# A two-layer conformer and attention trunk with grouped experts: the order of routing picks, of large experts' up splits, and GpSimd's share beside the routing

## The chip, the cores and the metric

The kernel runs on 1 core of a Trainium2 chip, as one program. Its time is the device time in microseconds, taken as the median of several runs. Five engines work side by side, each in the order of its own queue: TensorE (PE, with its weight loads as PEld), VectorE (DVE), ScalarE (ACT), GpSimd (POOL) and SyncE (SP), which only issues transfers and reads registers here. An instruction waits at the head of its engine's queue until its inputs are there, and everything queued behind it on that engine waits too.

## The reference, cut to what matters

512 tokens of width 1024 go through two layers. Each layer has a token mixer (layer 0: a conformer convolution; layer 1: differential attention over keys and values that are projected once) and then a mixture of 16 experts, of which each token uses two. Every part ends with a residual sum and a layer norm.

```
for l in range(2):
    mix = conformer_conv(x, ...) if l == 0 else diff_attention(x, k1, k2, v, ...)
    x = layer_norm(ALPHA * x + mix, ln_mix_g[l], ln_mix_b[l])
    # grouped_moe
    aff = sigmoid(x @ router_w); sel = aff + router_bias      # 4 groups of 4 experts
    group = argmax(sum of the two best sel of each group)
    e_idx = the two best experts of that group
    gates = one_hot(e_idx) * aff / (sum of the two aff)
    for e in range(16):
        h = silu(x @ w_gate[e]) * (x @ w_up[e])
        out += (h @ w_down[e]) * gates[:, e]
    x = layer_norm(ALPHA * x + out, ln_ffn_g[l], ln_ffn_b[l])
```

All inputs and the output are float32. Each expert's three weight matrices are 2 MB each.

## The kernel before, in words

**Precision.** Products that need it are made from two parts: a weight or an activation in float32 is split into a high part `hi` (a copy on ScalarE, L280) and a low part `lo` (the difference, on VectorE, L281), and a product is three matmuls (`mm3`, L283 to L286): hi by hi, hi by lo, lo by hi.

**Tiling.** Tokens are handled in four rows of 128 (`NT`). Layer 0's mixer ends in the product pw2, layer 1's in `project_out`; both accumulate a row of 128 x 1024 in two PSUM banks. `rows_out` (L1035 on) then adds the residual (L1040), transposes for the router (L1047), takes the logits (L1055), the statistics (L1062 to L1068), normalizes the row (L1084) and writes it out. For the last row, its first half is normalized by ScalarE and GpSimd instead (L1072 to L1081).

**Routing.** `route_tasks` (L352 on) computes for each row, in some 15 short VectorE instructions, which experts a token takes (`msk`), and with small matmuls (L395, L396) the place of each token in its expert's list (`pos`). Then `select_tasks` (L425 on) makes a one-hot matrix (L429) and TensorE picks expert 0's tokens out of the normalized rows: per row and half four matmuls (L439), accumulated over the four rows in banks 0 and 1; in total eight picks. The result is split to `xT0` (L1028, L1032), the input of expert 0. After the last row, `order_tasks` (L459 on) ranks the experts by their counts (`cnt`, L406; L467 to L477), and two small products (L481, L482) spread the order over all partitions, where VectorE copies it to `pii`, `pi` and `over` (L484 to L488). SP reads `pii` to find the weights of experts from the fourth on. `gates` (L411 to L415) are five VectorE steps that turn affinities into gate values; `arrange` (L492 on) uses them inside the expert stage.

**Who orders the mixers and the routing.** They are written as tasks of a planner (`Plan`, L109 on). A task has an engine, an estimated cost, what it reads and writes, and a priority. The planner takes the task that can begin first by its own estimates and, of those that can begin at once, the one with the lowest priority number; the engines' queues then hold that order. A pick is planned at 0.86 us (1.76 us with the zeroing of its bank), with priority 0; a mixer product at 0.645 to 1.29 us with priority 2. `first_parts` (L1099 on) splits the first two pieces of expert 0's gate weight within the plan, high parts on ScalarE (L1111) and low parts on GpSimd (L1112).

**Experts.** `moe` (L606 on) handles the experts in order of their counts. Experts 3, 5, 7, 9, 11 and 13 are small (64 places, unsplit float32 products); the others are large. A large expert: its gate product (`first_part`, with the transposes of the expert before it between its two halves), Silu, its up product (`product`, 24 matmuls), the multiplication, the transposes, the down product, a scaled copy to `y`, and a scatter from GpSimd that adds `y` to memory. There is one `y` buffer (`Y_BUFS = 1`). Weight splits use four `hi` and four `lo` buffers, just those of one weight. For a small expert e and the large one behind it, the order in the text is: gate product of e + 1, then small expert's down product with its copy to `y` and its scatter (`small_out`, L874 on: L879, L881, L882), then, in the next turn of the loop, the up weight of e + 1 is split and multiplied. Weights come as pieces of 1 MB through SP's queue (L251), at most three under way, up to 15 buffers ahead.

Of the kernel before, what the change touches and what calls it, by code (L numbers as in the profile page):

```python
# [11 lines left out]
F32 = mybir.dt.float32  # L12
# [4 lines left out]
ALU = mybir.AluOpType  # L17
# [178 lines left out]
def trunk(ctx: ExitStack, tc, x, a_w_pw1, a_b_pw1, a_w_dw, a_b_dw, a_ln_g, a_ln_b, a_w_pw2, a_b_pw2,  # L196
# [155 lines left out]
    def route_tasks(plan, b, R, room):  # L352
# [48 lines left out]
        if last:  # L401
            def total():
                for c in range(NT):
                    PE.matmul(pc[:, NT], ones16, msk[:, c], start=(c == 0), stop=(c == NT - 1))
            plan.add("PE", .2, total, [("route", c) for c in done], [("pc", NT)], 1)
            plan.add("DVE", .07, lambda: V.tensor_copy(R["cnt"], pc[:, NT, None, :].to_broadcast([P, 2, E])), [("pc", NT)], ["cnt"], 2)  # L406
            order_tasks(plan, R)
            g, m1 = o1, t4("gm1", [P, NT, 1])

            def gates():  # L410
                V.tensor_tensor(g, aff, msk, op=ALU.mult)  # L411
                V.tensor_reduce(m1, g, axis=AX.X, op=ALU.add)
                V.reciprocal(m1, m1)
                V.tensor_scalar(m1, m1, 1.0 / ALPHA, None, op0=ALU.mult)
                V.tensor_tensor(R["pg"][:, :, 1], g, m1.to_broadcast([P, NT, E]), op=ALU.mult)  # L415
            plan.add("DVE", 1.0, gates, [("route", c) for c in done], ["gates"], 9)
            plan.add("ACT", 1.3, lambda: A.activation(cp.tile([P, 1], F32, tag="sgl", name=nm("sgl")), aff[:, b, 0:1],
                                                      AF.Silu), [rk], ["table"], 3)
# [6 lines left out]
    def select_tasks(plan, b, R, z, zk, banks, late):  # L425
# [6 lines left out]
        for h in range(2):  # L432
            def pick(h=h):
# [4 lines left out]
                for j in range(4):  # L438
                    PE.matmul(banks[h][0][:, j], v[:, j], late["oh0"][:, b], start=False,  # L439
                              stop=(k == NT - 1 and j == 3))  # L440
            plan.add("PE", .86 + .9 * (k == 0), pick, [("oh", b), (zk, 0), (zk, 1)], [banks[h][1]], 0)
        plan.add("DVE", .2, lambda: V.tensor_tensor(
            late["oh1"][:, b], iota1, R["pos"][:, b, 1:2].to_broadcast([P, P]), op=ALU.is_equal),
            [("route", b), "late"], [("oh1", b), ("aT", 1), "rel"])
        if k == NT - 1:
# [8 lines left out]
            for h in range(2):  # L454
                ks = slice(4 * h, 4 * h + 4)
                split_tasks(plan, *(Later(lambda i=i, ks=ks: R["xT0"][:, i, ks]) for i in range(2)), banks[h][0], 512,
                            ("xT0", 0, h), ("xT0", 1, h), [banks[h][1], "xT0"])

    def order_tasks(plan, R):  # L459
# [20 lines left out]
        def arranged():  # L480
            PE.matmul(place_, ecol[0:E].to_broadcast([E, P]), hot[0:E, 0:E], start=True, stop=True)  # L481
            PE.matmul(of, kc[0:E, 1:2].to_broadcast([E, P]), hot[0:E, 0:E], start=True, stop=True)  # L482
        plan.add("PE", .4, arranged, ["hot"], [("pc", "pi")], 0)
        plan.add("DVE", .15, lambda: V.tensor_copy(pii, place_), [("pc", "pi")], ["pii"], 1)  # L484

        def rest():
            V.tensor_copy(pi, place_)
            V.tensor_tensor(over, of, caps, op=ALU.subtract)  # L488
        plan.add("DVE", .3, rest, [("pc", "pi")], ["pi"], 8)
        R.update(hot=hot, pi=pi, pii=pii, over=over)  # L490

# [114 lines left out]
    def moe(l, R, xsrc, ydst, more, order, first):  # L606

        with ExitStack() as st:
# [264 lines left out]

            def small_out(w, hs, yo, ixcol, gcol):  # L874
                acc = bank([P, 512])
                wd = [r.rearrange("p a b -> p (a b)").rearrange("p (j d) -> p j d", j=2) for r in w]
                for k in range(4):
                    for n in range(2):
                        PE.matmul(acc[64 * n:64 * (n + 1)], hs[:, k], wd[k // 2][:, k % 2, 512 * n:512 * (n + 1)],  # L879
                                  start=(k == 0), stop=(k == 3))  # L880
                A.activation(yo, acc, AF.Copy, scale=gcol)  # L881
                G.indirect_dma_start(out=half_view(ydst), out_offset=bass.IndirectOffsetOnAxis(ap=ixcol, axis=0),  # L882
# [82 lines left out]

            first_part(0)
            find_rows([0, 2], ohs)
            for e in range(E):
# [36 lines left out]
                if e in SMALL:  # L1005
                    small_out(weight(2, e), hT[e], new_y()[:, 512:1024], rows[e], gate[e])
                elif e < E - 1:
# [27 lines left out]
    def rows_out(plan, l, b, z, zk, acc, turned, logit, rx, norm, last=False):  # L1035
# [34 lines left out]
        for n in range(2):  # L1070
            zv = lambda n=n: z[:, zs[n]]
            if last and n == 0:  # L1072
                add("DVE", .07, lambda: V.scalar_tensor_tensor(
                    norm["nr"], norm["mv", b][:, 0:1], -1.0, norm["rs", b], op0=ALU.mult, op1=ALU.mult), [nk], ["nr"])
                add("ACT", .6, lambda zv=zv: A.activation(zv(), zv(), AF.Identity, scale=norm["rs", b][:, 0:1],
                                                          bias=norm["nr"][:, 0:1]), ["nr"], [(zk, n)], 1)

                def rest(zv=zv, n=n):
                    G.tensor_tensor(zv(), zv(), norm["g"][:, zs[n]], op=ALU.mult)
                    G.tensor_tensor(zv(), zv(), norm["b"][:, zs[n]], op=ALU.add)  # L1080
                add("POOL", 2.6, rest, ["ln_g", "ln_b"], [(zk, n)], 1)  # L1081
                continue
            for k, at, op in (("g", lambda: norm["mv", b], ALU.subtract), ("b", lambda: norm["rs", b], ALU.mult)):
# [15 lines left out]
    def first_parts(plan, pieces):  # L1099

        for i in range(2):
            for u in range(4):
                def part(k, u=u, i=i):
# [6 lines left out]
                    if not k:  # L1110
                        return A.activation(hi, src, AF.Copy)  # L1111
                    return G.tensor_tensor(lo, src, hi.bitcast(F32), op=ALU.subtract)  # L1112
                keys = [("hi", i, u // 2), ("lo", i, u // 2)]
                plan.add("ACT", .5, lambda part=part: part(0), [], [("raw", i), *keys], 3)
                plan.add("POOL", 1.25, lambda part=part: part(1), [], [("raw", i), keys[1]], 3)

# [884 lines left out]
```

## Time and profile before

| | |
|---|---|
| median of 3 runs | 1209.08 us (1207.22 to 1209.73) |
| profiled execution | 1207.24 us, span from first to last instruction 1205.5 us |
| PE busy | 1085.8 us (90%) |
| DVE busy | 786.0 us (65%) |
| ACT busy | 585.7 us (49%) |
| POOL busy | 323.6 us (27%) |
| mean granted TensorE clock | 0.954 |

A busy TensorE is not TensorE at its peak: matmuls are pipelined and their ends are modelled. The granted clock is the share of the full 2.4 GHz that TensorE was given; 0.5 is its lower level. In a timeline row stand the start and the duration in us, the engine, the line of the kernel, the operation, what it writes and reads, how many instructions were merged, and in brackets the idle time of the engine just before, with what ended it. By stages: layer 0's convolution runs to about 200 us, its routing to 264, its experts to about 560; the attention runs from there to about 847, its routing to 866, and layer 1's experts to about 1180.

### The profile page before, as it was taken

What the parts mean: (1) busy time and instruction counts of PE and PEld (TensorE: products, weight loads), DVE (VectorE), ACT (ScalarE), POOL (GpSimd) and SP (SyncE); (2) the same over time, 40 slices, a digit from 0 to 9 for tenths busy, and PEclk for the clock granted to TensorE, in tenths of its full rate; (3) what the DMA queues carried; (4) which work ended last, traced back from release to release, by engine and by line L of the source; (5) the groups of instructions that cost most, each with busy time, mean ns of one, the idle gap of its engine ahead of it and who ended that gap; (6) DMA issues with size and microseconds to landing.
All of it is one profiled execution on the core that took longest, in us unless ns stands there. A gap on an engine that the chain in (4) does not pass through costs nothing. (4 is left out here: it accounts for less than half of the span.)

```text
span 1205.5 us, 14628 instructions
## 1 busy us (share of the span) xinstructions
PE 1085.8 (90%) x5053; PEld 786.4 (65%) x5053; DVE 786.0 (65%) x1396; ACT 585.7 (49%) x932; POOL 323.6 (27%) x261
## 2 busy tenths in 40 slices
PE   6999769979999999967899999999699999898965
PEld 5888658867656665555677787688576556545632
DVE  4899974568866655467647738665598665544637
ACT  4556433137655545464346636542276555444631
POOL 2999941231112222012401101012311122110113
PEclk9999969979999999978999999999799999998998
DMA  8620335768999999958451131444589999999223
GB/s 249 208 71 1 138 108 87 276 225 286 360 361 366 372 372 385 389 186 262 151 146 36 36 105 71 175 140 164 193 314 356 393 386 375 381 395 383 81 71 125
DMA packets 80818, 276.58 MB, mean 229 GB/s; under 512 B 9691, under 2 KB 38725, under 8 KB 56150
## 3 DMA queue, kind: packets, MB, share of 16 engines
q1 hardware_dynamic: 72326, 259.44, 58.7%
q0 software_dynamic: 8256, 15.95, 5.6%
q8 instruction: 45, 0.74, 0.2%
q14 instruction: 47, 0.39, 0.1%
q10 hardware_dynamic: 144, 0.07, 0.0%
HBM read 258.62 MB, written 27.00 MB: 237 GB/s over the span
## 5 line engine op out<-in xcount | busy, mean ns | idle before, releaser
L281 DVE TENSOR_TENSOR lo<-raw,hi 128x1024 fp32r<-128x1024 f32 x232 | 280.3, 1230 | 121.5 <-ACT hi L280 118.8
L280 ACT ACTIVATE hi<-raw 128x1024 fp32r<-128x1024 f32 x236 | 244.7, 1058 | 86.6 <-PE mm L286 85.9
L284 PE MATMUL mm<-hi,xgh 128*128 128x512 f32 x288 | 122.0, 424 | 29.1 <-ACT hi L280 13.4
L285 PE MATMUL mm<-lo,xgh 128*128 128x512 f32 x288 | 119.3, 414 | 4.6 <-DVE lo L281 4.5
L286 PE MATMUL mm<-hi,xgl 128*128 128x512 f32 x288 | 118.0, 410 | 0.0
L1032 DVE TENSOR_TENSOR lo<-raw,hi 128x1024 fp32r<-128x1024 f32 x45 | 66.4, 1479 | 62.9 <-ACT hi L1028 62.3
L284 PE MATMUL all<-xh,hi 128*128 128x512 f32 x256 | 102.2, 399 | 0.2 <-ACT xh L1028 0.2
L285 PE MATMUL all<-xl,hi 128*128 128x512 f32 x256 | 99.9, 390 | 1.1 <-DVE xl L1032 1.1
L286 PE MATMUL all<-xh,lo 128*128 128x512 f32 x256 | 99.9, 390 | 0.0
L733 POOL DMA_INDIRECT ys<-y,ix x18 | 30.0, 1668 | 242.8 <-ACT y L732 189.3
L848 PE MATMUL mm<-raw,xgl 128*64 128x512 f32 x384 | 90.9, 599 | 0.0
L284 PEld LDWEIGHTS mm<-hi,xgh 128*128 128x128 f32 x288 | 56.7, 197 | 48.4 <-ACT hi L280 18.6
L1424 POOL TENSOR_TENSOR yconv<-yconv,prod 128x512 f32<-128x512 f32 x60 | 86.5, 1443 | 5.1 <-ACT yconv L1414 2.2
L1407 DVE SCALAR_TENSOR_TENSOR all<-hglu,wT,all 128x512 f32<-128x512 f32 x122 | 84.5, 752 | 2.6 <-ACT all L1393 1.8
L1421 ACT ACTIVATE prod<-hglu,wT 128x512 f32<-128x512 f32 x60 | 42.9, 721 | 60.0 <-POOL yconv L1424 54.7
L1810 POOL TENSOR_TENSOR fs<-fs,mhalf 128x1 f32<-128x1 f32 x32 | 19.4, 607 | 187.3 <-DVE fs L1808 187.1
L285 PEld LDWEIGHTS mm<-lo,xgh 128*128 128x128 f32 x288 | 56.6, 196 | 18.7 <-DVE lo L281 7.3
L286 PEld LDWEIGHTS mm<-hi,xgl 128*128 128x128 f32 x288 | 56.5, 196 | 16.1 <-DVE xgl L281 3.7
L286 PE MATMUL mm<-hi,hTl 128*128 128x512 f32 x160 | 63.9, 402 | 0.8 <-DVE hTl L281 0.8
L284 PE MATMUL mm<-hi,hTh 128*128 128x512 f32 x160 | 62.7, 411 | 1.5 <-ACT hTh L280 1.4
L285 PE MATMUL mm<-lo,hTh 128*128 128x512 f32 x160 | 64.0, 400 | 0.0
L1028 ACT ACTIVATE hi<-raw 128x1024 fp32r<-128x1024 f32 x52 | 54.3, 1054 | 12.9 <-DMA raw<-in_a_w_pw 10.0
(359 smaller groups left out, 2179.7 us busy)
## 6 DMA issues: line engine op xcount, KB each, us to landing
raw<-in_moe_w_gate SPq DMA_DIRECT2D x64, 1024.0 KB
raw<-in_moe_w_up SPq DMA_DIRECT2D x64, 1024.0 KB
raw<-in_moe_w_down SPq DMA_DIRECT2D x64, 1024.0 KB
raw<-in_a_w_pw SPq DMA_DIRECT2D x10, 1024.0 KB
raw<-in_w_kv SPq DMA_DIRECT2D x4, 1024.0 KB
raw<-in_w_kv SPq DMA_DIRECT2D x8, 512.0 KB
raw<-in_b_w_q SPq DMA_DIRECT2D x8, 512.0 KB
raw<-in_b_w_o SPq DMA_DIRECT2D x4, 1024.0 KB
```

The costliest lines, as they stand in the source:

```text
L280: nxt["high"] = A.activation(hi, src, AF.Copy).ins
L281: nxt["low"] = low.tensor_tensor(lo, src, hi.bitcast(F32), op=ALU.subtract).ins
L284: PE.matmul(acc, sh, mh, start=first, stop=False)
L285: PE.matmul(acc, sh, ml, start=False, stop=False)
L286: return PE.matmul(acc, sl, mh, start=False, stop=last).ins
L733: G.indirect_dma_start(out=ydst[:, :], out_offset=bass.IndirectOffsetOnAxis(ap=ixcol, axis=0), in_=y, in_offset=None, bounds_check=T - 1, ...
L848: PE.matmul(acc[at_:at_ + 64], xs[:, j, 64 * h:64 * (h + 1)], wm[h][:, j], start=(k == 0), stop=(k == KC - 1))
L1028: A.activation(now(hi), src, AF.Copy)
L1032: lambda: eng.tensor_tensor(now(lo), src, now(hi).bitcast(F32), op=ALU.subtract), sk + [hk], [lk],
L1407: add("DVE", .663, lambda v=v, dst=dst, src=src: V.scalar_tensor_tensor(dst, h[:, c, v:v + T], wT[:, c, v:v + 1], src, op0=ALU.mult, op1=A ...
L1421: add("ACT", .61, lambda v=v, p=p: A.activation(prod[p], h[:, c, v:v + T], AF.Copy, scale=wT[:, c, v:v + 1]), hk + wk, [("prod", p)], PRI[ ...
L1424: add("POOL", 1.3, lambda p=p: G.tensor_tensor(y[c], y[c], prod[p], op=ALU.add), [("prod", p)], [("y", c)], PRI["add"])
```

## The change

- `small_out` gets an instruction behind which its copy to `y` is issued. Where a small expert is followed by a large one, the large one's up weight is loaded and split (`halves_in`) just before `small_out`, and the copy is issued behind the last high part. The loop's later `product(weight(1, e), ...)` finds the split parts in `ahead`.
- The picks' priority goes from 0 to 3, below the mixer products' 2.
- The copy of the counts has priority 0 instead of 2.
- The gates' task is added behind the last split of `xT0` and waits for it.
- The two small products of `order_tasks` and the three copies behind them leave the plan; they are issued between the two halves of expert 0's gate product.
- The last row's first half is normalized by VectorE like every other half, and the low parts in `first_parts` are made by VectorE (priority 7) instead of GpSimd.

```diff
--- before.py
+++ after.py
@@ -403,7 +403,7 @@
                 for c in range(NT):
                     PE.matmul(pc[:, NT], ones16, msk[:, c], start=(c == 0), stop=(c == NT - 1))
             plan.add("PE", .2, total, [("route", c) for c in done], [("pc", NT)], 1)
-            plan.add("DVE", .07, lambda: V.tensor_copy(R["cnt"], pc[:, NT, None, :].to_broadcast([P, 2, E])), [("pc", NT)], ["cnt"], 2)
+            plan.add("DVE", .07, lambda: V.tensor_copy(R["cnt"], pc[:, NT, None, :].to_broadcast([P, 2, E])), [("pc", NT)], ["cnt"], 0)
             order_tasks(plan, R)
             g, m1 = o1, t4("gm1", [P, NT, 1])
 
@@ -413,7 +413,7 @@
                 V.reciprocal(m1, m1)
                 V.tensor_scalar(m1, m1, 1.0 / ALPHA, None, op0=ALU.mult)
                 V.tensor_tensor(R["pg"][:, :, 1], g, m1.to_broadcast([P, NT, E]), op=ALU.mult)
-            plan.add("DVE", 1.0, gates, [("route", c) for c in done], ["gates"], 9)
+            R["gating"] = lambda: plan.add("DVE", 1.0, gates, [("route", c) for c in done] + [("xT0", 1, 1)], ["gates"], 9)
             plan.add("ACT", 1.3, lambda: A.activation(cp.tile([P, 1], F32, tag="sgl", name=nm("sgl")), aff[:, b, 0:1],
                                                       AF.Silu), [rk], ["table"], 3)
 
@@ -438,7 +438,7 @@
                 for j in range(4):
                     PE.matmul(banks[h][0][:, j], v[:, j], late["oh0"][:, b], start=False,
                               stop=(k == NT - 1 and j == 3))
-            plan.add("PE", .86 + .9 * (k == 0), pick, [("oh", b), (zk, 0), (zk, 1)], [banks[h][1]], 0)
+            plan.add("PE", .86 + .9 * (k == 0), pick, [("oh", b), (zk, 0), (zk, 1)], [banks[h][1]], 3)
         plan.add("DVE", .2, lambda: V.tensor_tensor(
             late["oh1"][:, b], iota1, R["pos"][:, b, 1:2].to_broadcast([P, P]), op=ALU.is_equal),
             [("route", b), "late"], [("oh1", b), ("aT", 1), "rel"])
@@ -455,6 +455,7 @@
                 ks = slice(4 * h, 4 * h + 4)
                 split_tasks(plan, *(Later(lambda i=i, ks=ks: R["xT0"][:, i, ks]) for i in range(2)), banks[h][0], 512,
                             ("xT0", 0, h), ("xT0", 1, h), [banks[h][1], "xT0"])
+            R["gating"]()
 
     def order_tasks(plan, R):
 
@@ -480,13 +481,12 @@
         def arranged():
             PE.matmul(place_, ecol[0:E].to_broadcast([E, P]), hot[0:E, 0:E], start=True, stop=True)
             PE.matmul(of, kc[0:E, 1:2].to_broadcast([E, P]), hot[0:E, 0:E], start=True, stop=True)
-        plan.add("PE", .4, arranged, ["hot"], [("pc", "pi")], 0)
-        plan.add("DVE", .15, lambda: V.tensor_copy(pii, place_), [("pc", "pi")], ["pii"], 1)
-
-        def rest():
+        def places():
+            arranged()
+            V.tensor_copy(pii, place_)
             V.tensor_copy(pi, place_)
             V.tensor_tensor(over, of, caps, op=ALU.subtract)
-        plan.add("DVE", .3, rest, [("pc", "pi")], ["pi"], 8)
+        R["places"] = places
         R.update(hot=hot, pi=pi, pii=pii, over=over)
 
     def arrange(R, bank, room):
@@ -871,14 +871,15 @@
                 A.activation(hs, pt, AF.Copy)
                 return hs
 
-            def small_out(w, hs, yo, ixcol, gcol):
+            def small_out(w, hs, yo, ixcol, gcol, after=None):
                 acc = bank([P, 512])
                 wd = [r.rearrange("p a b -> p (a b)").rearrange("p (j d) -> p j d", j=2) for r in w]
                 for k in range(4):
                     for n in range(2):
                         PE.matmul(acc[64 * n:64 * (n + 1)], hs[:, k], wd[k // 2][:, k % 2, 512 * n:512 * (n + 1)],
                                   start=(k == 0), stop=(k == 3))
-                A.activation(yo, acc, AF.Copy, scale=gcol)
+                with tc.issue_after(after) if after else ExitStack():
+                    A.activation(yo, acc, AF.Copy, scale=gcol)
                 G.indirect_dma_start(out=half_view(ydst), out_offset=bass.IndirectOffsetOnAxis(ap=ixcol, axis=0),
                                      in_=yo, in_offset=None, bounds_check=2 * T - 1, oob_is_err=False,
                                      compute_op=ALU.add)
@@ -963,7 +964,7 @@
                 else:
                     sg[e] = gated(weight(0, e), xT[e], between)
 
-            first_part(0)
+            first_part(0, R["places"])
             find_rows([0, 2], ohs)
             for e in range(E):
                 if e + 1 < E:
@@ -1003,7 +1004,11 @@
                     with tc.issue_after(turned_x):
                         beyond_first(R, mp)
                 if e in SMALL:
-                    small_out(weight(2, e), hT[e], new_y()[:, 512:1024], rows[e], gate[e])
+                    wd, after = weight(2, e), None
+                    if e + 1 not in SMALL:
+                        ahead[1, e + 1] = halves_in(weight(1, e + 1))
+                        after = nxt["high"]
+                    small_out(wd, hT[e], new_y()[:, 512:1024], rows[e], gate[e], after)
                 elif e < E - 1:
                     expert_out(weight(2, e), *hT[e], rows[e], gate[e])
                 else:
@@ -1069,17 +1074,6 @@
         add("DVE", .3, lambda: negated_logits(l, lg[:, b], pl, norm["mv", b], norm["rs", b]), [nk, lk], [("lg", b)])
         for n in range(2):
             zv = lambda n=n: z[:, zs[n]]
-            if last and n == 0:
-                add("DVE", .07, lambda: V.scalar_tensor_tensor(
-                    norm["nr"], norm["mv", b][:, 0:1], -1.0, norm["rs", b], op0=ALU.mult, op1=ALU.mult), [nk], ["nr"])
-                add("ACT", .6, lambda zv=zv: A.activation(zv(), zv(), AF.Identity, scale=norm["rs", b][:, 0:1],
-                                                          bias=norm["nr"][:, 0:1]), ["nr"], [(zk, n)], 1)
-
-                def rest(zv=zv, n=n):
-                    G.tensor_tensor(zv(), zv(), norm["g"][:, zs[n]], op=ALU.mult)
-                    G.tensor_tensor(zv(), zv(), norm["b"][:, zs[n]], op=ALU.add)
-                add("POOL", 2.6, rest, ["ln_g", "ln_b"], [(zk, n)], 1)
-                continue
             for k, at, op in (("g", lambda: norm["mv", b], ALU.subtract), ("b", lambda: norm["rs", b], ALU.mult)):
                 add("DVE", .66, lambda zv=zv, n=n, k=k, at=at, op=op: V.scalar_tensor_tensor(
                     zv(), zv(), at()[:, 0:1], norm[k][:, zs[n]], op0=op, op1=ALU.mult if k == "g" else ALU.add),
@@ -1109,10 +1103,10 @@
                     src = raw_of[i][:, u]
                     if not k:
                         return A.activation(hi, src, AF.Copy)
-                    return G.tensor_tensor(lo, src, hi.bitcast(F32), op=ALU.subtract)
+                    return V.tensor_tensor(lo, src, hi.bitcast(F32), op=ALU.subtract)
                 keys = [("hi", i, u // 2), ("lo", i, u // 2)]
                 plan.add("ACT", .5, lambda part=part: part(0), [], [("raw", i), *keys], 3)
-                plan.add("POOL", 1.25, lambda part=part: part(1), [], [("raw", i), keys[1]], 3)
+                plan.add("DVE", .66, lambda part=part: part(1), [], [("raw", i), keys[1]], 7)
 
     raw_of = {}
```

## Rows read from the trace of the kernel before

**Rows 1.** Page, busy time by engine, and transfer engines' busy tenths in 40 slices.

```profile
PE 1085.8 (90%) x5053; PEld 786.4 (65%) x5053; DVE 786.0 (65%) x1396; ACT 585.7 (49%) x932; POOL 323.6 (27%) x261
...
DMA  8620335768999999958451131444589999999223
```

**Rows 2.** Stretches: length, busy us (instructions) by engine, granted clock, DMA share, GB/s.

```profile
222.46:241.60 19.14, 19.14 (x95) 16.72 (x93) 9.31 (x19) 4.83 (x9) 6.62 (x6) 1.00 0.58 218
241.60:263.61 22.01, 13.78 (x73) 13.06 (x73) 17.65 (x48) 5.87 (x10) 11.39 (x10) 0.69 0.79 287
846.65:865.96 19.31, 8.39 (x55) 7.80 (x55) 14.62 (x42) 5.25 (x9) 8.78 (x8) 0.71 0.67 228
```

**Rows 3.** Timeline of TensorE, two up products behind a small expert.

```profile
514.38 0.79 PE L284 MATMUL mm<-hi,xgh 128*128 128x512 f32 x1 [3.11 <-ACT hi L280]
...
1126.94 0.50 PE L284 MATMUL mm<-hi,xgh 128*128 128x512 f32 x1 [1.78 <-ACT hi L280]
```

**Rows 4.** Timeline of ScalarE, small experts' copies to y, and one run of splits.

```profile
346.78 0.69 ACT L881 ACTIVATE y<-mm,sgate 128x512 f32<-128x512 f32 x1 [2.25 <-PE mm L879]
...
512.70 0.69 ACT L881 ACTIVATE y<-mm,sgate 128x512 f32<-128x512 f32 x1 [4.38 <-DMA ys<-y,ix]
513.28 3.89 ACT L280 ACTIVATE hi<-raw 128x1024 fp32r<-128x1024 f32 x4
...
1046.05 0.69 ACT L881 ACTIVATE y<-mm,sgate 128x512 f32<-128x512 f32 x1 [4.99 <-DMA ys<-y,ix]
...
1086.98 0.69 ACT L881 ACTIVATE y<-mm,sgate 128x512 f32<-128x512 f32 x1 [6.81 <-DMA ys<-y,ix]
...
1125.26 0.69 ACT L881 ACTIVATE y<-mm,sgate 128x512 f32<-128x512 f32 x1 [3.05 <-PE mm L879]
```

**Rows 5.** Stretches of five up products of large experts, columns as in rows 2.

```profile
511.27:523.36 12.09, 8.51 (x25) 6.49 (x26) 5.86 (x5) 7.65 (x9) 1.56 (x1) 0.72 0.81 291
1043.80:1055.08 11.28, 7.75 (x26) 5.41 (x25) 3.50 (x3) 4.01 (x5) 2.64 (x2) 0.85 1.00 368
1083.11:1097.14 14.03, 8.02 (x26) 5.78 (x24) 4.63 (x4) 4.47 (x5) 1.59 (x1) 0.76 1.01 380
1125.16:1135.20 10.04, 7.50 (x26) 5.85 (x26) 5.86 (x5) 7.65 (x8) 1.55 (x1) 0.83 0.09 11
947.34:953.12 5.78, 5.78 (x27) 4.39 (x26) 2.65 (x3) 4.06 (x5) 2.62 (x2) 1.00 1.01 375
```

**Rows 6.** Timeline of TensorE in the two routing stages.

```profile
231.01 3.77 PE L439 MATMUL all<-oh,xt 128*128 128x128 f32 x16
...
263.07 0.39 PE L481 MATMUL all<-rank,cs 16*128 16x16 f32 x2 [1.99 <-DVE rank L477]
...
263.61 0.50 PE L284 MATMUL mm<-hi,xT 128*128 128x512 f32 x1
...
857.39 0.17 PE L396 MATMUL all<-msk,tri 128*128 128x16 f16 x1 [6.96 <-DVE msk L387]
```

**Rows 7.** Timeline of VectorE in the two routing stages.

```profile
241.59 1.20 DVE L371 TENSOR_TENSOR before<-gs 128x16 f32<-128x16 f32 x1
...
246.89 0.74 DVE L1084 SCALAR_TENSOR_TENSOR xt<-xt,ln_mv,g 128x512 f32<-128x512 f32 x1
...
252.27 1.23 DVE L381 TENSOR_TENSOR sel<-aff,rb 128x16 f32<-128x16 f32 x1
...
254.73 0.17 DVE L371 TENSOR_TENSOR before<-gs 128x16 f32<-128x16 f32 x1
...
853.63 1.30 DVE L374 TENSOR_TENSOR before<-before,cs 128x64 f32<-128x64 f32 x1
```

**Rows 8.** ScalarE's waits from 890 to 1130 us, grouped: total, times, longest.

```profile
ACT hi L280 <- PE mm L286: 18.9, 40, 1.2
```

**Rows 9.** Timeline of SP's queue, loads of two up weights.

```profile
489.26 2.83 SPq L251 DMA_DIRECT2D raw<-in_moe_w_up  x2
...
1054.44 3.46 SPq L251 DMA_DIRECT2D raw<-in_moe_w_up  x2
```

## The prediction

> **What bounds the kernel now.** I read the page first. TensorE is busy for 90% of the span, and the transfer engines show nines in both expert stages [rows 1]. So two resources could set the pace there, and gaps on TensorE are worth something only where no load sets it. Next I cut the span into stretches: in the two stages where a layer is routed, TensorE is busy 13.78 of 22.01 us and 8.39 of 19.31 us, at a granted clock of 0.69 and 0.71; just ahead of the first it is busy 19.14 of 19.14 us at 1.00 [rows 2]. The reader is to see three different limits in a row: TensorE full, then a chain of short VectorE steps, then experts. Inside the experts I listed what TensorE waits for. Four waits stand out, all at the first up product of a large expert behind a small one, all for ScalarE's high part of the up weight (the first and the last of them: [rows 3]). ScalarE's own row just ahead names the cause [rows 4]: it stood at the small expert's copy (L881), in three cases for the scatter of the previous `y` (one buffer), in the fourth for TensorE's own small product. The first row of that group is one of the eight other places of this kind: there the copy waits 2.25 us for the small product, and TensorE lost nothing.
>
> **The up splits ahead of the copy.** Removed: the four waits. The price of each is read over a whole up product of 24 matmuls, because the clock also falls afterwards: 12.09, 11.28, 14.03 and 10.04 us, at granted clocks of 0.72 to 0.85, against 5.78 us at 1.00 for the undisturbed one [rows 5]. The excesses are 6.31, 5.50, 8.25 and 4.26, together 24.3 us. Behind the change ScalarE goes from the gate's Silu straight to four splits (3.89 us for the four [rows 4]), and only then to the copy. The gate product has by then read all four hi and lo buffers, so the splits wait for nothing. In the first case they would begin at about 508.3 and the first low part would be done near 510.6, before TensorE ends the small product at 511.27. What is late next: the copy itself still waits for its scatter until 512.70, 1046.05 and 1086.98 [rows 4], and behind it on ScalarE stand the splits of the next weight. Those need buffers that the up product begins to give back a quarter of 5.78 us after its start, so they lose up to 2 to 3 us, but they are wanted only when the up product and, twice, two small products are through. I take 2 us off for this: 22 us. Bounds: 0 (the wait moves with the copy) to 24.3. In the eight other places the copy comes about 1 us later than now; its scatter has a whole large expert until `y` is wanted again, so I cost that at nothing; without this cover it would be 1 us each, 8 us. The loads of the up weights keep their place in SP's queue, behind the small expert's down weight, so nothing moves there.
>
> **Picks below products.** Before the change the picks of earlier rows stand in TensorE's queue ahead of the last row's products: 3.77 us for two picks at full clock [rows 6] (a pick is one half of one row), twice that and the zeroing of two banks in layer 0 before 241.60. TensorE has no idle time there [rows 2], so the last product ends earlier by what is put behind it, 7 to 9 us, and the picks fall into the waits of the last row's chain. Work is only moved, so the gain cannot exceed TensorE's idle time behind the last product: 22.01 - 13.78 = 8.2 us in layer 0 and 19.31 - 8.39 = 10.9 us in layer 1. The 6.96 us wait for `msk` [rows 6] is the largest single piece. The loss side: planned at 0.86, a pick really takes 1.9 us, and each may stand ahead of the last row's transposes, logits or counts.
>
> **No GpSimd tensors beside the routing.** While GpSimd runs a two-input tensor instruction, VectorE steps of the chain are stretched: the same subtraction took 1.20 us and 0.17 us, a 128x16 addition 1.23 us, in layer 1 a 128x64 comparison 1.30 us [rows 7]. In layer 0 seven instructions from 241.59 to 252.27 carry about 6.2 us of such excess; in layer 1 three between 852.3 and 856.1 carry 2.8 us. Added to VectorE, per layer: eight low parts and two more normalization steps of 128x512, priced by the row of 0.74 us, minus one tiny step: 7.2 us. So VectorE has no less to do (17.65 of 22.01 us busy before [rows 2]); what changes is that the new pieces have priority 7 and 1 and fall between the chain's steps, whereas the stretches fell on them. Bounds: minus 7.2 us per layer if all of it lies on the chain, plus 6.2 and 2.8 us if none does. I take this as the means by which the idle time above can be filled, not as a further term.
>
> **Places inside the first gate product; counts and gates.** TensorE now waits 1.99 us for `rank` ahead of the first gate matmul [rows 6], and a like wait stands in layer 1. Both are part of the idle time already counted. The two small products move behind twelve matmuls, where the ranks are long done; the 0.54 us from their start to the first gate matmul come back there. The gates' five VectorE steps (about 1 us) move behind the last split, where VectorE next waits for TensorE; if that cover is gone they cost 1 us per layer. SP reads the experts' order later too, but the first load that needs it also waits for a raw buffer, which the splits of the following up weight give back later still.
>
> **The sum.** Of the idle 8.2 and 10.9 us I take 6 and 7, since a chain with hand-overs between five engines is never filled entirely, and 1 us per layer for a first gate product that begins at the full clock, 15 us in all (bounds: minus 7 per layer to plus 10 and 13). With 22 that is 37 us. The profiled execution took 1207.24 us (span 1205.5 us); the median of the runs is 1.8 us above it. 1207.2 - 37 = 1170 by the first, 1172 by the second: I say 1171.
>
> **Rivals.**
> *Loads set the pace in the experts* (0.12). Three of the four excess stretches have the transfer engines at 0.81 to 1.01 [rows 5]. If loads bounded them, the 13.75 us of the second and third case would come back as waits for weights further on, and 37 becomes 23: 1184. Against it: in the grouped waits of ScalarE over layer 1's experts no load of weights appears, and the splits' own entry is for TensorE freeing a buffer [rows 8]; and the up pieces are asked for long before use: issued by 492.1 and split at 513.3, issued by 1057.9 and split at 1087.6 [rows 4, 9]. Less about 7.5 us until they land (an estimate: three in flight at some 2.5 us each), 13 and 22 us of lead, of which the change uses 5 and 13. The Trainium skill, "Trainium Architecture — The Big Picture", section "What this means for kernel authors", gives a memory bandwidth of about 360 GB/s per core; the second and third stretch, at 368 and 380 GB/s [rows 5], lie at that figure, so by this rule the stage is at the memory's limit and this rival would hold. Saturated transfers and a starved consumer are two things, and the trace so far shows only the first.
> *VectorE becomes the routing's bound* (0.17). The 7.2 us of added steps eat what the picks free; routing gives nothing, the splits give 22: 1185. For it: VectorE is already busy 80% of that stretch. Against it: TensorE's products end earlier, which spreads VectorE's load.
> *The change doesn't move the splits* (0.06): the compiler's order keeps something that waits ahead of them on ScalarE. Only routing gains 15: 1192.
> *Slower* (0.06): the picks stand in series behind the last product, without its being earlier, because it waits for inputs rather than for TensorE's queue. Three rows' picks at 3.77 us and VectorE's 7.2 us per layer make 2 x 18.5 = 37 us; minus 22 for the splits and 4 for the rank waits, the time is 1218. It turns slower once more than 26 of the 37 us lie on the path. Against it: no idle TensorE ahead of the last product [rows 2].
>
> **How the numbers follow.** My forecast has 0.56, the rivals 0.41, and 0.03 is for gains and losses that cancel. The range runs from 1158 (all 24.3 and the full idle time with its clock) to 1192 (splits not moved); it holds the first two rivals. No change means within 0.2%, some 2.4 us, about what a measurement of this kernel can tell from none. Faster: 0.91; no change: 0.03; slower: 0.06.
>
> **What would show it.** Splits: L881 behind four splits, no wait for them at an up product behind a small expert, four up products of about 6 us. Picks: no pick matmuls between the last row's products; more of both routing stretches busy, first gate matmul 6 to 7 us nearer to the start of the stretch. GpSimd: no chain step of 128x16 over 0.7 us. Wrong, if TensorE's waits for high parts turn into waits for `raw` loads, or if VectorE is busy without a break from the last product to the picks.

## The result, and the profile after

The kernel after takes 1169.55 us (median of 4 runs, 1165.97 to 1172.35) against 1208.9 us before, in the same rounds: a ratio of 0.9675, 95% interval 0.9644 to 0.9705. The forecast was 1171 us in 1158 to 1192. The profiled executions took 1207.24 us (span 1205.5) and 1170.88 us (span 1169.1), so the traces hold 36.4 of the 39.4 us between the medians.

Moments of TensorE that both traces have (first start of each kind of matmul, or end of the last product) show where the lead is won:

| moment | before, us | after, us | earlier by |
|---|---|---|---|
| mixer's first product, layer 0 | 177.84 | 178.72 | -0.9 |
| last product ahead of the experts, layer 0 | 241.60 | 232.95 | 8.7 |
| first gate matmul, layer 0 | 263.61 | 257.27 | 6.3 |
| mixer's first product, layer 1 | 572.55 | 561.42 | 11.1 |
| first gate matmul, layer 1 | 865.96 | 844.07 | 21.9 |
| end of the span | 1205.5 | 1169.1 | 36.4 |

So layer 0's routing gave 6.3 + 0.9 = 7.2 us, layer 0's experts 4.8, layer 1 up to its first gate matmul 10.8, layer 1's experts and the tail 14.5. The last number is small because the profile of the kernel before has a short tail: from the end of its last small product to the end of the span it took 42.0 us, while in the profiles of e2 and e3 below, whose experts' code is the same, that took 44.9 and 44.7 us (43.4 in the kernel after).

The page of the kernel after, busy time by engine and the transfer engines' tenths, beside [rows 1]:

```profile
PE 1085.1 (93%) x5053; PEld 786.9 (67%) x5053; DVE 783.1 (67%) x1414; ACT 584.4 (50%) x930; POOL 299.8 (26%) x241
...
DMA  8620244866999999988461230534779999999632
```

TensorE does the same work in a shorter span, and GpSimd has 24 us less. The four up products behind a small expert, from the end of the small product to the end of the up product, beside the first four of [rows 5]:

```profile
504.48:510.28 5.80, 5.80 (x26) 4.71 (x26) 3.89 (x4) 4.60 (x5) 2.41 (x1) 1.00 0.98 350
1022.24:1028.52 6.28, 6.28 (x29) 4.92 (x30) 2.57 (x3) 1.71 (x3) 3.01 (x2) 1.00 0.98 381
1057.73:1063.53 5.80, 5.80 (x25) 4.44 (x26) 2.66 (x3) 1.52 (x2) 0.39 (x1) 1.00 0.96 346
1091.48:1097.29 5.81, 5.81 (x26) 4.72 (x26) 3.89 (x4) 4.61 (x5) 1.77 (x1) 1.00 1.01 391
```

12.09, 11.28, 14.03 and 10.04 us have become 5.80, 6.28, 5.80 and 5.81 at the full clock: 23.75 us (the second window now also holds four transposes, x29). A fifth place gained too, one of the eight others, in layer 0. Before, TensorE stood twice in it:

```profile
477.79 0.49 PE L284 MATMUL mm<-hi,xgh 128*128 128x512 f32 x1 [0.23 <-ACT hi L280]
479.08 0.50 PE L285 MATMUL mm<-lo,xgh 128*128 128x512 f32 x1 [0.80 <-DVE lo L281]
```

The stretch from the small product to the end of the up product, before and after:

```profile
475.41:483.24 7.83, 6.80 (x31) 4.85 (x29) 3.53 (x3) 4.05 (x5) 2.65 (x2) 1.00 0.98 352
470.05:476.45 6.40, 6.40 (x30) 4.84 (x29) 2.82 (x3) 3.07 (x4) 3.12 (x2) 1.00 0.91 353
```

ScalarE's timeline at the first of them and at two others, beside [rows 4]:

```profile
501.43 3.89 ACT L280 ACTIVATE hi<-raw 128x1024 fp32r<-128x1024 f32 x4
505.22 0.68 ACT L882 ACTIVATE y<-mm,sgate 128x512 f32<-128x512 f32 x1
...
1025.13 0.69 ACT L882 ACTIVATE y<-mm,sgate 128x512 f32<-128x512 f32 x1 [2.36 <-DMA ys<-y,ix]
...
1092.83 0.69 ACT L882 ACTIVATE y<-mm,sgate 128x512 f32<-128x512 f32 x1 [0.51 <-DMA ys<-y,ix]
1093.42 2.17 ACT L280 ACTIVATE hi<-raw 128x1024 fp32r<-128x1024 f32 x2
```

The copy (now L882) stands behind four splits and still waits for the scatter now and then, by at most 3.6 us, but TensorE waits for none of the splits behind it. The two routing stages, from the last product to the first gate matmul, beside [rows 2]:

```profile
232.95:257.27 24.32, 21.29 (x109) 19.83 (x109) 14.89 (x57) 5.57 (x10) 3.62 (x4) 0.78 0.74 265
822.99:844.07 21.08, 20.72 (x106) 19.42 (x106) 13.45 (x42) 4.86 (x9) 1.70 (x2) 0.84 0.82 293
```

TensorE was busy 13.78 of 22.01 and 8.39 of 19.31 us; now all but 3.0 and 0.4 us are busy, since the picks lie here. TensorE's own rows, at the end of layer 0's routing and of layer 1's, beside [rows 6]:

```profile
249.65 0.17 PE L396 MATMUL all<-msk,tri 128*128 128x16 f16 x1
...
255.21 0.60 PE L482 MATMUL all<-rank,cs 16*128 16x16 f32 x2
255.66 0.58 PE L483 MATMUL all<-rank,kc 16*128 16x16 f32 x2
257.27 0.80 PE L284 MATMUL mm<-hi,xT 128*128 128x512 f32 x1 [1.03 <-DVE xT L1037]
...
830.18 7.71 PE L439 MATMUL all<-aT,ob 128*128 128x128 f32 x32
837.72 0.22 PE L395 MATMUL all<-msk,ones 128*128 128x16 f16 x3
...
843.11 0.61 PE L482 MATMUL all<-rank,cs 16*128 16x16 f32 x2
843.56 0.58 PE L483 MATMUL all<-rank,kc 16*128 16x16 f32 x2
844.07 0.80 PE L284 MATMUL mm<-hi,xT 128*128 128x512 f32 x1
```

The waits for `rank` and `msk` are gone. But the order's two products (L482, L483) still stand ahead of the first gate matmul. VectorE, beside [rows 7]:

```profile
247.62 0.17 DVE L371 TENSOR_TENSOR before<-gs 128x16 f32<-128x16 f32 x1
...
256.28 0.17 DVE L486 CAST pii<-all 128x16 int32<-128x16 f32 x1 [2.69 <-PE all L483]
...
256.53 1.28 DVE L1037 TENSOR_TENSOR xT<-all,xT 128x512 fp32r<-128x512 f32 x2
...
835.22 0.17 DVE L387 SCALAR_TENSOR_TENSOR msk<-rank,grank 128x16 f16<-128x16 f32 x1
```

The chain's steps are back to about 0.2 us; only one of layer 0 is longer (0.56 us). In layer 0 the low parts of the first expert's input (L1037) stand behind a copy of the order (L486), which waits for TensorE. And in layer 1 the counts come at 837.72, 2.3 us after `msk` is done, behind four picks (7.71 us).

### The profile page after: what moved, and what is told of

Read it like the earlier page. It is cut to its first block, busy times and chain, and to the rows that moved or that the text cites. A ratio compares the mean times of both kernels' runs of the same rounds, so it can differ in the third digit from the quotient of the medians.

```text
span 1169.1 us, 14618 instructions
## 1 busy us (share of the span) xinstructions
PE 1085.1 (93%) x5053; PEld 786.9 (67%) x5053; DVE 783.1 (67%) x1414; ACT 584.4 (50%) x930; POOL 299.8 (26%) x241
## 5 line engine op out<-in xcount | busy, mean ns | idle before, releaser
L285 PE MATMUL mm<-lo,xgh 128*128 128x512 f32 x288 | 116.8, 405 | 1.3 <-DVE lo L281 1.2
L1037 DVE TENSOR_TENSOR lo<-raw,hi 128x1024 fp32r<-128x1024 f32 x45 | 66.4, 1479 | 63.1 <-ACT hi L1033 62.6
```

What stands on the lines that cost most here:

```text
L285: PE.matmul(acc, sh, ml, start=False, stop=False)
L1037: lambda: eng.tensor_tensor(now(lo), src, now(hi).bitcast(F32), op=ALU.subtract), sk + [hk], [lk],
```

## The experiments

All are timed beside the kernel before. Ratios are to it, with 95% intervals; the medians of before were 1210.3 (e1 to e3, e10), 1210.7 (e4, e8, e9, e11) and 1208.2 us (e6, e12 to e14).

| run | median, us | ratio |
|---|---|---|
| e1 splits alone | 1185.99 | 0.9802 (0.9789 to 0.9815) |
| e2 routing alone | 1194.79 | 0.9858 (0.9836 to 0.9880) |
| e3 picks alone | 1196.95 | 0.9895 (0.9878 to 0.9912) |
| e10 GpSimd moves alone | 1204.27 | 0.9944 (0.9931 to 0.9958) |
| e4 after, GpSimd moves undone | 1171.58 | 0.9669 (0.9646 to 0.9692) |
| e6 after, small edits undone | 1171.08 | 0.9682 (0.9662 to 0.9702) |
| e8 after, places in their own bank | 1165.43 | 0.9618 (0.9593 to 0.9643) |
| e11 after, pick priced at 1.8 | 1167.80 | 0.9643 (0.9620 to 0.9667) |
| e12 e8 and e11 together | 1161.69 | 0.9611 (0.9590 to 0.9632) |
| e13 after, once more | 1168.02 | 0.9664 (0.9640 to 0.9687) |
| e9 after, 9.4 MB more | 1166.16 | 0.9635 (0.9610 to 0.9661) |
| e14 after, 37.7 MB more | 1221.02 | 1.0096 (1.0073 to 1.0119) |

**e1, the splits alone** (the kernel before with `small_out`'s part of the change).

```
+    with tc.issue_after(after) if after else ExitStack():     # in small_out
+        A.activation(yo, acc, AF.Copy, scale=gcol)
...
+    if e + 1 not in SMALL:
+        ahead[1, e + 1] = halves_in(weight(1, e + 1))
+        after = nxt["high"]
+    small_out(wd, hT[e], ..., gate[e], after)
```

> The kernel before with the first part of the change alone: the large expert's up splits ahead of the small expert's copy. My theory (each of the four waits is ScalarE's order, and no load is late behind it): the four excesses less about 2 us, so 22 to 23 us less than before, about 1186 us, with four up products of 6 us. Rival (loads set the pace in the experts): only the first and the fourth place give, some 9 to 11 us, about 1199 us, and new waits for raw weights appear. Rival (the two parts of the change need each other): under 15 us less.

Measured 24.3 us less (22.4 to 25.5 by the interval). The splits need nothing of the routing's edits, and the whole excess comes back: the four up products take 5.8, 6.4, 5.8 and 5.8 us in its trace, and no load is late behind them. That is the case against the first rival, at all four places.

**e2, the routing's edits alone** (the kernel after without the lines above).

> The kernel after without the up splits: all that is changed about the routing. My theory: 15 us less than before, 13 to 17, about 1194 us, 6 of it in layer 0 and 10 in layer 1 by the first gate product. Rival (VectorE's added 7.2 us per layer eat what the picks free): within 2 us of before.

15.5 us less (14.5 to 19.8). With e1 that makes 39.8 us, against 39.4 for both at once: the two parts add.

**e3, the picks alone** (the kernel before, one number).

```
-    plan.add("PE", .86 + .9 * (k == 0), pick, ..., [banks[h][1]], 0)
+    plan.add("PE", .86 + .9 * (k == 0), pick, ..., [banks[h][1]], 3)
```

> The kernel before with one number changed: the picks rank below the mixer's last products. My theory (picks fill TensorE's idle time; the GpSimd stretches stay on the chain and cost part of it): 8 to 12 us less than before, about 1199 us. Rival (the picks only stand in series behind the products, and GpSimd's stretches were what cost): within 3 us of before, or slower.

13.4 us less (10.7 to 14.8), a little above the 8 to 12 that were expected. The last product ends at 233.18 and 828.22 instead of 241.60 and 846.64, and TensorE fills what follows, by the windows from there to the first gate matmul, GpSimd's tensors (last engine column) still beside it:

```profile
233.18:257.65 24.47, 21.23 (x110) 19.24 (x109) 18.77 (x54) 6.20 (x11) 13.28 (x12) 0.86 0.73 256
828.22:851.75 23.53, 20.84 (x107) 19.56 (x106) 13.78 (x42) 5.75 (x10) 12.11 (x11) 0.80 0.71 255
```

The waits for `rank` are still there, one in each layer:

```profile
257.11 0.39 PE L481 MATMUL all<-rank,cs 16*128 16x16 f32 x2 [1.13 <-DVE rank L477]
...
850.78 0.61 PE L481 MATMUL all<-rank,cs 16*128 16x16 f32 x2 [2.24 <-DVE rank L477]
```

**e10, the GpSimd moves alone** (the kernel before with the low parts and the two normalization steps on VectorE).

```
-    return G.tensor_tensor(lo, src, hi.bitcast(F32), op=ALU.subtract)
+    return V.tensor_tensor(lo, src, hi.bitcast(F32), op=ALU.subtract)
-    plan.add("POOL", 1.25, ..., 3)
+    plan.add("DVE", .66, ..., 7)      # and rows_out without its `last and n == 0` branch
```

> The kernel before with only GpSimd's two-input tensor instructions beside the routing moved to VectorE. My theory (with the picks still ahead of the last products TensorE is the bound up to the last product, and behind it the stretches cost 6.2 and 2.8 us of which the moved steps take back half): 2 to 6 us less than before, about 1205 us. Rival (all of the stretch lies on the chain and the added steps on none): 9 us less. Rival (VectorE full): 0 to 5 us slower.

6.0 us less (5.1 to 8.4), the upper end of what was expected. From the last product to the first gate matmul it is 19.18 and 17.39 us instead of 22.01 and 19.31; in layer 0 part of that is lost ahead of it, since the last product ends at 243.16 instead of 241.60. e3 and e10 together would be 19.4 us; e2, which holds both, gives 15.5. That points to one idle time on which both draw, but e2's interval reaches 19.8; e4 decides it.

**e4, the GpSimd moves undone in the kernel after** (the reverse of that diff).

> The kernel after with GpSimd's two-input tensor instructions beside the routing put back, all else as it is. Theory A (picks and GpSimd moves fill the same wait, so with the picks moved the GpSimd part has little left): 0 to 3 us more than the kernel after, some 1171 us, and VectorE's stretched steps are back in the trace without TensorE waiting longer for them in layer 1. Theory B (the two parts are independent, worth 6 us as it is alone): 6 us more, about 1176 us.

Not to be told from the kernel after (ratios 0.9669 against 0.9675 and, in e13, 0.9664); a loss of 6 us, 0.005 in the ratio, would be more than these intervals allow. The stretched VectorE steps are back, as in layer 1, with GpSimd's instructions beside them:

```profile
831.11 1.23 DVE L381 TENSOR_TENSOR sel<-aff,rb 128x16 f32<-128x16 f32 x1
832.38 1.25 DVE L371 TENSOR_TENSOR before<-sel 128x64 f32<-128x64 f32 x1
...
830.57 1.75 POOL L1085 TENSOR_TENSOR ob<-ob,b 128x512 f32<-128x512 f32 x1
832.27 1.27 POOL L1117 TENSOR_TENSOR lo<-raw,hi 128x512 fp32r<-128x512 f32 x1
```

But TensorE is busy 20.87 of 21.32 us between layer 1's last product and the gate, as before the undoing (20.72 of 21.08): what was 6 us alone is worth nothing measurable once the picks lie there. The Trainium skill, "SBUF — State Buffer", section "Who interferes with whom", says that a VectorE instruction with two SBUF inputs contends with a GpSimd instruction that reads SBUF; these rows agree (1.25 against 0.22 us for the same comparison in the kernel after). Here such a stretch no longer lies on the path.

**e6, the small edits undone** (places in the plan again, counts at rank 2, gates ahead of the picks; each as in the change's diff, reversed).

> The kernel after with the three small edits undone: the order's products and copies in the plan again, counts at rank 2, gates ahead of the picks. Theory (the products never moved inside the gate product, so only the counts and the gates' 1 us count): 1 to 2 us more than the kernel after. Rival by the prediction (the rank waits and 0.54 us come back in each layer): 4 us or more. Rival: they do nothing, or are slower, since the plan would have put the products in an idle place: within 1 us.

3 us more than the kernel after of the same set (e13), but the intervals overlap: at most a few microseconds, not separated. The trace shows two effects against each other. In layer 1 TensorE waits for `rank` again, and from the last product to the gate it is 23.32 us instead of 21.08:

```profile
836.74 0.27 PE L467 MATMUL all<-ident,cnt 128*32 128x1 f32 x2
839.30 0.60 PE L481 MATMUL all<-rank,cs 16*128 16x16 f32 x2 [2.29 <-DVE rank L477]
```

The product of the counts (L467) comes behind the last pick here; in the kernel after it comes ahead of it. In layer 0 the gate product does not wait for `xT`, and the stretch is 22.95 us instead of 24.32 (23.83 in e13).

**e8, the order's products in a bank of their own** (in the kernel after).

```
-    col, place_, of = pc[0:n, 0, E:E + 1], pc[:, 1, E:n], pc[:, 2, E:n]
+    col = pc[0:n, 0, E:E + 1]
     def places():
-        arranged()
+        room = tbank([P, 2, E]); place_, of = room[:, 0], room[:, 1]
+        ...                                  # the same two matmuls
```

> The kernel after with the two products of the experts' order written to a PSUM tile of the experts' stage, instead of the routing's. Theory: the routing's bank keeps the first gate product from starting ahead of them, so they were never inside it; with their own bank they come behind twelve matmuls, the low parts of the first expert's input no longer stand behind their copies on VectorE, and the first gate matmul comes about 1.5 us sooner in layer 0 and 0.5 to 1 us in layer 1: 1.5 to 2.5 us less than the kernel after, about 1167.5 us. Rival (the order of the matmuls stays or the clock takes it back): within 0.5 us.

4.1 us less than the kernel after by the medians of two sets (ratios 0.9618 and 0.9675, whose intervals just part; those of e8 and e13 just overlap, and e12 settles it). TensorE goes from the last pick straight into the gate product:

```profile
252.65 2.21 PE L439 MATMUL all<-oh,xt 128*128 128x128 f32 x8
254.52 0.78 PE L284 MATMUL mm<-hi,xT 128*128 128x512 f32 x1
...
837.30 2.21 PE L439 MATMUL all<-aT,ob 128*128 128x128 f32 x8
839.17 0.78 PE L284 MATMUL mm<-hi,xT 128*128 128x512 f32 x1
```

From the last product to the gate it is 21.80 and 19.84 us instead of 24.32 and 21.08: 2.5 and 1.2 us (2.0 and 1.2 against e13's 23.83 and 21.08). In TensorE's queue the two products now come behind twelve gate matmuls:

```profile
258.45 0.39 PE L484 MATMUL tp<-rank,cs 16*128 16x16 f32 x2
258.70 0.37 PE L485 MATMUL tp<-rank,kc 16*128 16x16 f32 x2
```

Nothing else was changed, so it was their tile in the routing's PSUM bank that held them ahead. By which rule it did so is not shown: in layer 1 of the kernel after, the gate product begins at 844.07, before VectorE reads that bank at 845.32.

**e11, the planner's price of a pick** (in the kernel after).

```
-    plan.add("PE", .86 + .9 * (k == 0), pick, ...
+    plan.add("PE", 1.8 + .9 * (k == 0), pick, ...
```

> The kernel after with the planner's price of a pick at 1.8 in place of 0.86, near what the trace shows; the last row's counts then pass two more picks. Theory A (behind the last product TensorE is now full with picks in layer 1, 20.72 of 21.08 us busy, so their order is worth little there, and in layer 0 only part of the 3 idle us): 0 to 1.5 us less than the kernel after. Theory B (the counts that stand 2.6 us behind picks set the end): 2.5 us less in each layer, 5 us in all, about 1165 us.

In TensorE's queue the last row's counts pass one more pick in layer 1 and none in layer 0, not two, and in layer 1 they come 1.6 us after `msk` is done. The time is the same as that of the kernel after within the intervals (0.9643 against 0.9675 and 0.9664), but these are too wide to rule out theory B's 5 us. From the mixers' first products to the first gate matmuls the trace has 78.0 and 281.2 us, the kernel after 78.6 and 282.7 (79.1 and 282.3 in e13): some 2 us in all, nearer to theory A.

**e12, both** (e8's and e11's lines).

> The kernel after with both edits: the order's products in a bank of their own, and the planner's price of a pick at 1.8. Theory (the one saves at the front of the gate product, the other ahead of the last counts, so they add): some 6 us less than the kernel after, about 1163 us. Rival (TensorE is full of picks either way, so the pick's price has nothing left to give once the gate product starts right behind them): as with the bank alone, 1165 us.

The fastest version here, 6.3 us below the kernel after of the same set, with intervals that part (0.9590 to 0.9632, 0.9640 to 0.9687). Against e8 alone (0.9618) it isn't separated, nor against e11 (0.9643): the two together are shown to gain, and most of it is put down to the bank by e8's trace. TensorE is now busy 20.00 of 20.36 and 19.21 of 19.21 us in the two stretches: this stage has almost no idle time left to fill.

**e13, the kernel after again.**

> The kernel after once more, on the same chip and in the same rounds as the others of this set: 1169 us, so that the sets can be compared.

1168.02 us. Its profiled execution took 1165.58 us, the first one 1170.88; what lies between is told at the end.

**e9 and e14, more bytes** (in the kernel after; e14 copies 2 MB each).

```
+    if k == 2 and e not in SMALL and e < E - 1:
+        S.dma_start(spare[:, :], moe_w_down[l, 0, 0:P])
```

> The kernel after with 0.5 MB more moved behind each large expert's down weight but the last (a copy in memory that nothing reads), 18 times, 9.4 MB in all. Theory A (loads have a lead in the experts and TensorE sets the pace): within 3 us of the kernel after, or at most 8. Theory B (loads set the pace there, as the rival of the prediction has it): 9.4 MB at the 380 GB/s of the stretches are 25 us more, about 1194 us, and TensorE waits for high parts of which ScalarE waits for raw weights.

> The kernel after with 2 MB more moved behind each large expert's down weight but the last, 18 times, 37.7 MB in all. If the stretches of 370 to 394 GB/s are the most that the transfers move, each layer's experts, which read some 110 MB in 295 us, cannot take 19 MB more for nothing: 50 us more in each layer at 380 GB/s, less the slack that is there, so 80 to 100 us more. If the pace is TensorE's and transfers have much room, under 20 us more.

Both failed as tests of the experts. Nothing makes such a copy wait, and SP issued all 18 long before the experts; e9's and then e14's, with the first and the last start:

```profile
L933 SPq DMA_DIRECT2D spare<-in_moe_w_down x18: 488/488/646, 51.6 to 127.3; - x18
```

```profile
L933 SPq DMA_DIRECT2D spare<-in_moe_w_down x18: 488/488/646, 51.6 to 204.7; - x18
```

In e14 TensorE waits 57.4 us for another load (`rh`) at the end of layer 0's mixer, and that is the run's 53 us:

```profile
PE all L1491 <- DMA rh<-in_relhot: 57.4, 1, 57.4
```

How much more the experts' stages could move stays open; that they are not short of bytes rests on e1.

## Why the prediction was right, point by point

**The bound.** Three limits in a row, as read. The time moved in both places where TensorE had waited.

**The splits.** Forecast 22 us, bounds 0 to 24.3. Measured 23.75 in the four windows and 24.3 alone (e1). The mechanism held step by step. The 2 us that I took off for the late copy were not lost where I put them: of the next weight's splits none makes TensorE wait. Two other things were not in the forecast, and nearly cancel. The eight other places did not only cost nothing, as said; the fifth place gained 1.4 us, and no wait of TensorE for a high part of an up weight is left in either layer. And from layer 0's last such up product to layer 1's mixer it took 49.2 to 49.8 us in the four profiles without the splits and 50.2 to 51.7 in the ten with them; what makes it longer was not followed.

**Picks.** Forecast 13 us (6 and 7) as the idle time behind the last product that could be filled. e3 gives 13.4 alone. The bound by idle time was the right way to size it: 8.2 and 10.9 us were there; 3.2 and 2.7 are left in e3, 3.0 and 0.4 in the kernel after. The share of each layer was off: the whole change fills 5.2 us in layer 0 and 10.5 in layer 1. The reason given for 7 of 10.9, that such a chain is never filled entirely, is one that no run shows; in layer 1 nearly all of it was. The loss named there, picks ahead of the last counts, did happen in layer 1 (2.3 us); what it is worth is not separated from nothing (e11).

**GpSimd.** This step failed as the prediction put it: "the means by which the idle time above can be filled". The picks fill it without these moves (e3: 13.4 of e2's 15.5 us), and with the picks moved the moves can be taken back at no measurable cost (e4). They are a second way to the same time: 6 us alone, little behind the first. The bounds, minus 7.2 to plus 6.2 and 2.8 us, hold it.

**Places, counts and gates.** "The two small products move behind twelve matmuls" was wrong: they are issued there in the program's text but stand ahead of the gate product on TensorE, and in layer 0 the low parts of `xT` stand behind their copies. I read the order of issue from the code and didn't ask what the compiler must keep in order; the bank that the products write decides it (e8). So the 0.54 us did not come back, and 1.03 us of a new wait for `xT` came in layer 0. The rank waits did go, but not by that move: with the picks alone they stay (e3, 1.13 and 2.24 us), and with the small edits undone layer 1's comes back (e6, 2.29 us), where the counts' product stands behind the last pick. So the small edits gain some 2 us in layer 1 and lose about 1 in layer 0; the times do not separate them from nothing (e6), and which of the three gains was not tried. The gates were hidden, as said: no wait for them shows in the trace.

**The clock.** One microsecond per layer for a gate product that begins at the full clock: in the first profile it does not begin so. The first matmuls take 0.63 us instead of 0.40 for 3.2 us in layer 0 and 3.5 in layer 1 (4.0 and 5.7 before). Their starts lie 0.43 us apart instead of 0.23, so by an estimate from these rows the change gave back 0.4 and 1.0 us. In e13, the same kernel, layer 0's gate product is at the full clock from its start and layer 1's again is not. The term was taken as a gain of the change; in layer 0 it is chance, as the last section shows.

**The sum.** 37 us forecast; 36.4 between the profiles and 39.4 between the medians. Taken apart, the splits gave 24.3 us (e1) against 22 and the routing 15.5 (e2) against 15. The first was too low by the 2 us for the late copy. The second agrees in part by luck: layer 0's idle time and the clock were taken too high, layer 1's idle time too low.

**The rivals.** Loads: the stretches run at 346 to 391 GB/s and TensorE waits for no weight there. The Trainium skill, "Trainium Architecture — The Big Picture", section "What this means for kernel authors", gives about 360 GB/s per core; two of the four stretches, at 381 and 391, exceed it. What decided was whether anybody waited. In ScalarE's grouped waits over layer 1's experts (868 to 1092 us) the weights now appear once, 1.2 us, where [rows 8] had none:

```profile
ACT hi L280 <- PE mm L286: 20.4, 44, 1.0
...
ACT hi L280 <- DMA raw<-in_moe_w_gate: 1.2, 1, 1.2
```

VectorE as the bound: it is busy 14.89 of 24.32 us in layer 0's routing and 13.45 of 21.08 in layer 1's, less than TensorE. Splits not moved: they moved. The slower one: the last product did end sooner, by 8.7 us.

## What to carry to other kernels

Price a wait over the whole product behind it, clock included, and ask what the waiting engine's queue holds ahead of it; moved work is worth at most the idle time it can fall into, and a second edit that aims at the same idle time adds little. When code is moved to another place in the program, ask which buffer still ties it to the old one, and look for it there in the trace before counting its gain.

## What was not expected of the hardware

The same program ran layer 0's first gate and up products at two clocks in two executions. The kernel after in its first profile and in e13, from the first gate matmul to the next expert's first product, with the one wait in between:

```profile
257.27:277.19 19.92, 18.57 (x76) 15.27 (x77) 11.02 (x21) 9.80 (x13) 1.27 (x1) 0.75 0.45 161
...
266.56 0.63 PE L501 MATMUL mm<-rank,y 32*128 32x32 f32 x4 [1.35 <-ACT y L499]
```

```profile
257.02:272.46 15.44, 14.09 (x76) 11.83 (x77) 10.63 (x21) 9.70 (x13) 1.27 (x1) 1.00 0.46 157
...
264.86 0.63 PE L501 MATMUL mm<-rank,y 32*128 32x32 f32 x4 [1.35 <-ACT y L499]
```

4.5 us lie between them (the kernel before took 18.71 us, at a clock of 0.82), at the same waits: in both TensorE stands 1.35 us for `y`. In the first profile the matmuls take 0.63 us instead of 0.40 at two places, the start of the gate product and behind that wait, which cost 1.4 and 3.0 us; in e13 they take 0.40 us throughout. These are the lower and the higher of the two clocks (1.2 and 2.4 GHz). That is most of the 5.4 us between the two spans, and it is larger than several of the edits tried here. What decides which clock is granted was not found out; so a term of some microseconds is to be read from medians and from the waits in a window, not from the spans of two profiles.
